# Scaling the sink-attention weights on ScalarE, one tile for all sink columns, and earlier steps from projection to scores

## The chip, the cores and the metric

The kernel runs on one core of a Trainium2 chip. The metric is the device time of one execution in microseconds (us); lower is better. TensorE (PE) does the matmuls and transposes, with its weight loads (PEld) overlapping them; VectorE (DVE), ScalarE (ACT) and GpSimd (POOL) do the rest, and SyncE (SP) issues the weight loads from memory.

## The reference

Two transformer blocks of width 1024 on 256 tokens. The first is an FFN, a mixer of dilated-window and block attention, and an FFN. The second has two layers with modulated norms; the change lies in the mixer of its first layer, sliding-window attention with a sink:

```python
    qkv = h @ w_qkv                       # 16 query heads, 2 key/value heads, 64 wide
    q = partial_rope(rmsnorm_2(q, q_gain), positions)
    k = partial_rope(rmsnorm_2(k, k_gain), positions)
    ...
    s = jnp.where(valid, s, -jnp.inf)
    sink_col = jnp.broadcast_to(sink_logit, s.shape[:-1] + (1,))
    p = jax.nn.softmax(jnp.concatenate([s, sink_col], axis=-1), axis=-1)[..., :-1]
    o = jnp.einsum('bkgqs,bskd->bqkgd', p.astype(vb.dtype), vb)
    ...
    x = x + g1 * (out @ w_o)              # sliding-window layer, then its FFN
```

## The kernel before

Every weight matrix is read once from memory in blocks of sixteen 128x128 tiles (`raw`). ACT rounds a block to a high part (`wh`, line 211, in quarters of 128x512) and DVE subtracts to get the low part (`wl`, line 219). Each product is three matmuls (`mm3`, lines 271 to 273). TensorE's instruction stream is written out by the Python code, and so is every other engine's: a manual schedule, in which each engine runs its list strictly in the order written.

What runs beside the matmuls is a set of coroutines in the list `hooks`. The code that emits matmuls calls `pump()` after every four products (12 matmuls); a pump advances each coroutine by one step and casts at most a quarter or two of a coming weight block. So a step written one pump earlier lands 12 matmuls earlier in TensorE's stream.

The mixer of the sink attention, from 600 us to 679 us, goes so:

- `feat_unit` projects two 128-row column tiles of q, k or v at a time (16 products, four pumps). Five units: (k, q0), (v, q1), (q2, q3), (q4, q5), (q6, q7). Its `evac` calls `shifted`: DVE multiplies by the norm's root (`sh`, line 988), ACT adds the shift (`flat`, line 991), and `operand` follows as a coroutine: TensorE turns the tile (line 1029), ACT squares it (`hsq`, 1046), DVE multiplies by the gain (`ht`, 1047) and reduces (`hss`, 1049), POOL does the rotation and the root (1051 to 1057), TensorE turns it back (1061) and ACT writes `qT` or `kT` (1067, 1065).
- `soft_heads` works on eight pairs of heads, called pair 0 to pair 7 here. `run_heads` starts a pair every second pump when its q tile is ready, and holds at most `most` pairs alive. The steps of a pair: scores on TensorE (line 691, tiles `at`) with mask and row minimum on DVE (`u`, `lo`, line 703); exponentials with row sums on ACT (line 711); reciprocals and scaling by them on DVE (lines 717, 719); the turn of the weights on TensorE (line 726) and copies to `pt` on ACT (line 728); two pumps later the product with the values (line 736), `yh` on ACT (750), then `yl` on DVE (752), and two pumps on the pair is `ready`.
- `out_proj` multiplies by w_o, K tile by K tile: K tile c needs pair c, takes eight products (two pumps), and while pair c is not ready the code only calls `pump()`, with no matmul in between. Here such a pump is called an empty pump.

The PSUM tiles `at` share four banks, which the code hands out as they come free. A tile's first write waits until the readers of the bank's last tile are done. Which tile follows which is in the built program.

A separate coroutine, `two_norms`, takes the roots of two norms, spreads them over the partitions, and after a pause multiplies the residual `xT` by one of them on POOL (line 978), one of eight tiles per pump.

Of the kernel before, what the change touches and what calls it, by code (L numbers as in the profile page):

```python
# [2 lines left out]

# [7 lines left out]
F32 = mybir.dt.float32  # L11
# [7 lines left out]
S = 256  # L19
# [8 lines left out]

SWA_HEADS = 2, 3, (1, 1, 2)
MOBA_HEADS = 6, 2, (1, 1, 1)  # L30
# [127 lines left out]
def hybrid_two_block_kernel(ctx: ExitStack, tc: tile.TileContext, x, w, ada, vecs, rows, pos, consts,  # L158
# [400 lines left out]

    def feat_unit(name, xh, xl, evac, n=S, first=False):  # L560

        wh, wl = W.next(name)
        ps = [mm_ps([128, n]), mm_ps([128, n])]
        order = [(u, kc) for u in range(2) for kc in range(DC)]
        if first:
            order.sort(key=lambda o: o[1])
        for i, (u, kc) in enumerate(order):
            t = u * DC + kc
            mm3(ps[u], wh[:, t], wl[:, t], xh[:, kc, :n], xl[:, kc, :n], kc == 0, kc == DC - 1)
            if i % 4 == 3:  # L570
                pump()
            if i == 11:
                release()
        held.extend((evac, u, ps[u]) for u in range(2))
        if not first:
            release()
# [77 lines left out]
    def soft_heads(pool, n_heads, n_parts, part, y_h, y_l, ready, sink=None, gate=lambda j: True,  # L654
# [6 lines left out]
        cut = 128 + (sink is not None)  # L661
        wide = 384 + 2 * (sink is not None)

        def one(c):
# [15 lines left out]
            for j in js:  # L680
                u[j] = pool.tile([128, n_parts, wide], F32, tag=f"u{n_parts}", bufs=2 * most, name=nm("u"))
                lo[j] = pool.tile([128, 2 * n_parts], F32, tag=f"lo{n_parts}", bufs=2 * most, name=nm("lo"))
                sums[j] = pool.tile([128, 2], F32, tag="sm", bufs=6, name=nm("sm"))
                if sink is not None:
                    nc.vector.tensor_copy(u[j][:, 0, 128:386:257], sink[:, j:j + 1].to_broadcast([128, 2]))
            for g in range(n_parts):
# [22 lines left out]
            for j in js:  # L709
                for tt, sl in ((0, slice(0, cut)), (1, slice(cut, wide))):  # L710
                    nc.scalar.activation(u[j][:, :, sl], u[j][:, :, sl], AF.Exp,
                                         bias=lo[j][:, 2 * g + tt:2 * g + tt + 1],
                                         scale=-1.0, accum_out=sums[j][:, tt:tt + 1])
            yield from pause(gaps[0])
            for j in js:
                rs = pool.tile([128, 2], F32, tag="rs", bufs=6, name=nm("rs"))
                nc.vector.reciprocal(rs, sums[j])
                for tt, sl in ((0, slice(0, 128)), (1, slice(cut, cut + 256))):
                    nc.vector.tensor_scalar(u[j][:, :, sl], u[j][:, :, sl], rs[:, tt:tt + 1], None, op0=ALU.mult)
            yield from pause(gaps[1])  # L720
# [31 lines left out]
            nc.vector.tensor_sub(y_l[:, c], o, y_h[:, c])  # L752
            yield
            yield
# [205 lines left out]
    def two_norms():  # L960
# [14 lines left out]
        fin.spread(r4[:, 0:2], fin.r)  # L975
        yield from pause(14)
        for d in range(DC):
# [4 lines left out]

    def shifted(pool, norm, p, dst, then):

# [9 lines left out]

        hooks.append(rest())

# [16 lines left out]
    with ExitStack() as mix:  # L1013
# [11 lines left out]
        def operand(c, flat):  # L1025
# [21 lines left out]
            nc.vector.tensor_mul(t, p, R[:, at:at + 64].unsqueeze(1).unsqueeze(1).to_broadcast([128, 2, 2, 64]))  # L1047
            yield
            nc.vector.tensor_reduce(ss, sq, axis=mybir.AxisListType.X, op=ALU.add)
# [31 lines left out]
        def keep(two):  # L1081
            def evac(u, p):
                t = mp.tile([128, S], F32, tag="flat", bufs=4, name=nm("flat"))
                shifted(mp, pre, p, t, operand(two[u], t))
            return evac

        for i, two in enumerate(SWA_UNITS):
            feat_unit("wqkv_a_2", xgh, xgl, keep(two), S + 2, first=i == 0)
            if i == 1:
                hooks.append(soft_heads(mp, 16, 1, swa_part, yh, yl, ready, nsink, gate, *SWA_HEADS, lambda: 9 in done))  # L1090
# [177 lines left out]
```

## Time and profile before

| what | value |
|---|---|
| median of three runs | 1189.0 us (1188.76 to 1190.79) |
| the profiled execution: its own time, its span | 1188.8 us, 1187.0 us |
| TensorE busy over the span | 1169.7 us (99%) |
| VectorE, ScalarE, GpSimd busy | 964.4 us, 620.9 us, 129.4 us |
| granted TensorE clock | full speed in all 40 slices |
| from 606.30 to 678.84 us (72.54 us): PE, DVE, ACT, POOL busy | 68.19, 57.91, 51.56, 33.92 us |

The span runs from the first to the last instruction that the profiler saw; about 1.8 us of the execution's time lie outside it. A matmul's record overlaps the next one's, so TensorE counts as busy unless a wait is longer than the overlap. A row by stretch gives the stretch and its length, the busy time of PE, PEld, DVE, ACT and POOL, then the granted clock, the busy share of the DMA engines and GB/s.

### The profile page before, as it was taken

To read this page: it belongs to the slowest core of one execution; us is meant where nothing else is said; L and a number is where in the kernel's file an instruction comes from. 1 tells how busy PE (TensorE), PEld (TensorE's weight loads), DVE (VectorE), ACT (ScalarE), POOL (GpSimd) and SP (SyncE) were. 2 spreads that over 40 slices of the span, in tenths; PEclk is the share of its full clock that TensorE was granted. 3 is DMA by queue.
4 is the path that set the end of the run, shared out by engine and by line. 5 is a ranking of instruction groups with operands and counts; after the bars stand their busy time and mean duration, and the time that the engine had idled before them with its cause. 6 is when DMAs were issued, how large, how long until landed. Compare 5 with 4: busy or idle time off the path is not lost. (4 is left out here: it accounts for less than half of the span.)

```text
span 1187.0 us, 24693 instructions
## 1 busy us (share of the span) xinstructions
PE 1169.7 (99%) x9762; PEld 1132.9 (95%) x9762; DVE 964.4 (81%) x2070; ACT 620.9 (52%) x1324; POOL 129.4 (11%) x166
## 2 busy tenths in 40 slices
PE   8999999999999999999998999999999999999998
PEld 7999999999889999999996899999998889999998
DVE  7989987566567999999878799999968877988752
ACT  5555444455546554554467765444546666545541
POOL 5000001220202200001247010000100002000000
PEclk9999999999999999999999999999999999999999
DMA  8876765535343768876551267767653335755450
GB/s 310 318 276 261 271 241 191 208 126 178 108 142 138 254 253 326 323 277 242 178 185 72 99 252 307 290 264 315 249 191 127 123 131 181 288 218 178 163 203 27
DMA packets 45331, 251.73 MB, mean 212 GB/s; under 512 B 5280, under 2 KB 8096, under 8 KB 21536
## 3 DMA queue, kind: packets, MB, share of 16 engines
q1 hardware_dynamic: 44784, 248.78, 57.2%
q8 instruction: 77, 1.26, 0.4%
q10 hardware_dynamic: 432, 1.38, 0.4%
q14 instruction: 38, 0.31, 0.1%
HBM read 249.09 MB, written 1.05 MB: 211 GB/s over the span
## 5 line engine op out<-in xcount | busy, mean ns | idle before, releaser
L211 ACT CAST wh<-raw 128x512 fp32r<-128x512 f32 (+1 forms) x752 | 420.2, 613 | 265.8 <-issue 138.4
L219 DVE TENSOR_TENSOR wl<-raw,wh 128x512 fp32r<-128x512 f32 x744 | 501.1, 707 | 51.8 <-ACT wh L211 50.5
L271 PE MATMUL mm<-xgh,wh 128*128 128x256 f32 (+1 forms) x1840 | 524.8, 285 | 0.0
L273 PE MATMUL mm<-xgh,wl 128*128 128x256 f32 (+1 forms) x1840 | 519.3, 282 | 0.0
L272 PE MATMUL mm<-xgl,wh 128*128 128x256 f32 (+1 forms) x1840 | 518.0, 282 | 0.0
L271 PEld LDWEIGHTS mm<-xgh,wh 128*128 128x128 f32 x1840 | 347.0, 189 | 7.5 <-issue 7.0
L272 PEld LDWEIGHTS mm<-xgl,wh 128*128 128x128 f32 x1840 | 348.3, 189 | 0.0
L273 PEld LDWEIGHTS mm<-xgh,wl 128*128 128x128 f32 x1840 | 347.1, 189 | 0.2 <-DVE wl L219 0.2
L271 PE MATMUL mm<-ah,wh 128*128 128x256 f32 x704 | 197.1, 280 | 0.0
L272 PE MATMUL mm<-al,wh 128*128 128x256 f32 x704 | 196.7, 279 | 0.0
L273 PE MATMUL mm<-ah,wl 128*128 128x256 f32 x704 | 196.7, 279 | 0.0
L272 PEld LDWEIGHTS mm<-al,wh 128*128 128x128 f32 x704 | 132.2, 188 | 0.0
L271 PEld LDWEIGHTS mm<-ah,wh 128*128 128x128 f32 x704 | 132.0, 188 | 0.1
L273 PEld LDWEIGHTS mm<-ah,wl 128*128 128x128 f32 x704 | 131.9, 187 | 0.0
L340 POOL TENSOR_TENSOR ssq<-ssq,sq 128x256 f32<-128x256 f32 x49 | 41.2, 847 | 688.7 <-ACT sq L335 687.8
L439 DVE SCALAR_TENSOR_TENSOR acc<-ada,cs,acc 128x1024 f32<-128x1024 f32 x84 | 107.5, 1280 | 0.6
L335 ACT ACTIVATE sq<-xT 128x256 f32<-128x256 f32 x49 | 19.7, 412 | 83.3 <-DVE xT L554 74.8
L494 DVE TENSOR_TENSOR tu<-mm,rB 128x256 f32<-128x256 f32 x80 | 33.5, 419 | 23.8 <-PE mm L273 23.7
L507 ACT CAST ah<-a 128x256 fp32r<-128x256 f32 x88 | 35.4, 405 | 20.6 <-DVE a L505 13.5
L500 ACT ACTIVATE sg<-tg,bb 128x256 f32<-128x256 f32 x44 | 22.4, 508 | 32.3 <-DVE bb L498 31.8
L272 PE MATMUL at<-xgl,wh 128*128 128x256 f32 (+1 forms) x128 | 37.2, 291 | 1.6 <-DVE xgl L377 1.4
L509 DVE TENSOR_TENSOR al<-a,ah 128x256 fp32r<-128x256 f32 x88 | 36.5, 419 | 1.9 <-ACT ah L507 1.9
(200 smaller groups left out, 1398.3 us busy)
## 6 DMA issues: line engine op xcount, KB each, us to landing
raw<-in_w SPq DMA_DIRECT2D x185, 1024.0 KB, 5.2
ada<-in_ada SPq DMA_DIRECT2D x96, 512.0 KB, 4.7
raw<-in_w SPq DMA_DIRECT2D x8, 128.0 KB, 4.0
raw<-in_w SPq DMA_DIRECT2D x4, 256.0 KB, 5.2
out<-xT SPq DMA_DIRECT2D x8, 128.0 KB, 2.1
xT<-in_x SPq DMA_DIRECT2D x3, 256.0 KB, 4.3
M<-in_masks ACTq DMA_DIRECT2D x1, 768.0 KB, 4.3
Mstick<-in_masks ACTq DMA_DIRECT2D x1, 386.0 KB, 3.3
```

The costliest lines, as they stand in the source:

```text
L211: nc.scalar.copy(h[:, part], self.raw[i][:, part])
L219: engine.tensor_sub(l[:, part], self.raw[i][:, part], h[:, part])
L271: nc.tensor.matmul(ps, lhsT=lh, rhs=rh, start=start, stop=False)
L272: nc.tensor.matmul(ps, lhsT=lh, rhs=rl, start=False, stop=False)
L273: nc.tensor.matmul(ps, lhsT=ll, rhs=rh, start=False, stop=stop)
L335: nc.scalar.activation(t, src, AF.Square, scale=scale)
L340: nc.gpsimd.tensor_add(self.ssq, self.ssq, t)
L439: nc.vector.scalar_tensor_tensor(self.acc, raw, self.cs[:, kc:kc + 1], self.acc, op0=ALU.mult, op1=ALU.add)
L494: nc.vector.tensor_mul(tu, ps[1][:, :S], norm.r)
L500: nc.scalar.activation(sg, tg, AF.Silu, bias=bb[:, 0:1] if shift else 0.0)
L507: nc.scalar.copy(ah[:, c], a)
L509: nc.vector.tensor_sub(al[:, c], a, ah[:, c])
```

## The change

Six edits, all in or around the sink attention.

1. All sixteen heads get their weights in one tile, `wells`, and both sink columns of all heads are written by one copy before the first pair starts, where before two small copies per pair wrote them.
2. The two reciprocals of a pair come in one pump, and the scaling follows in the next, on ACT (`AF.Copy` with the reciprocal as scale), where before both stood in one pump on DVE. Heads without a sink keep their scaling on DVE, after both reciprocals.
3. The last idle step before `ready` is taken out, for all three users of `soft_heads`.
4. `operand` reduces in the pump in which it squares; ACT's `flat` is issued as soon as `sh` is (the turn still comes two pumps on); the first unit's tiles are released one pump sooner (`free=7`).
5. `SWA_HEADS` lets four pairs live at once (before, three).
6. `two_norms` pauses 20 pumps (before, 14) ahead of the eight products on POOL.

```diff
-SWA_HEADS = 2, 3, (1, 1, 2)
+SWA_HEADS = 2, 4, (1, 1, 2)
...
-    def feat_unit(name, xh, xl, evac, n=S, first=False):
+    def feat_unit(name, xh, xl, evac, n=S, first=False, free=11):
...
-            if i == 11:
+            if i == free:
                 release()
...
+        if sink is not None:
+            wells = pool.tile([128, n_heads, wide], F32, name="wells")
+            nc.vector.tensor_copy(wells[:, :, 128:386:257], sink.unsqueeze(2).to_broadcast([128, n_heads, 2]))
...
-                u[j] = pool.tile([128, n_parts, wide], F32, tag=f"u{n_parts}", bufs=2 * most, name=nm("u"))
+                if sink is None:
+                    u[j] = pool.tile([128, n_parts, wide], F32, tag=f"u{n_parts}", bufs=2 * most, name=nm("u"))
+                else:
+                    u[j] = wells[:, j:j + 1]
...
-                if sink is not None:
-                    nc.vector.tensor_copy(u[j][:, 0, 128:386:257], sink[:, j:j + 1].to_broadcast([128, 2]))
...
+            rs = {j: pool.tile([128, 2], F32, tag="rs", bufs=6, name=nm("rs")) for j in js}
             for j in js:
-                rs = pool.tile([128, 2], F32, tag="rs", bufs=6, name=nm("rs"))
-                nc.vector.reciprocal(rs, sums[j])
+                nc.vector.reciprocal(rs[j], sums[j])
+            if sink is not None:
+                yield
+            for j in js:
                 for tt, sl in ((0, slice(0, 128)), (1, slice(cut, cut + 256))):
-                    nc.vector.tensor_scalar(u[j][:, :, sl], u[j][:, :, sl], rs[:, tt:tt + 1], None, op0=ALU.mult)
+                    if sink is None:
+                        nc.vector.tensor_scalar(u[j][:, :, sl], u[j][:, :, sl], rs[j][:, tt:tt + 1], None, op0=ALU.mult)
+                    else:
+                        nc.scalar.activation(u[j][:, :, sl], u[j][:, :, sl], AF.Copy, scale=rs[j][:, tt:tt + 1])
...
             nc.vector.tensor_sub(y_l[:, c], o, y_h[:, c])
             yield
-            yield
             ready.add(c)
...
-        yield from pause(14)
+        yield from pause(20)
...
-    def shifted(pool, norm, p, dst, then):
+    def shifted(pool, norm, p, dst, then, at_once=False):
...
-        hooks.append(rest())
+        g = rest()
+        if at_once:
+            next(g)
+            g = chain(pause(1), g)
+        hooks.append(g)
...
             nc.vector.tensor_mul(t, p, R[:, at:at + 64].unsqueeze(1).unsqueeze(1).to_broadcast([128, 2, 2, 64]))
-            yield
             nc.vector.tensor_reduce(ss, sq, axis=mybir.AxisListType.X, op=ALU.add)
...
-                shifted(mp, pre, p, t, operand(two[u], t))
+                shifted(mp, pre, p, t, operand(two[u], t), True)
...
-            feat_unit("wqkv_a_2", xgh, xgl, keep(two), S + 2, first=i == 0)
+            feat_unit("wqkv_a_2", xgh, xgl, keep(two), S + 2, first=i == 0, free=7)
```

What this does to the order shows in three places. In the rows, the line numbers of the changed kernel are larger by 5 to 14, and the number behind a name tells one buffer from another.

**TensorE where the projections end and the output projection begins.** In the kernel before, the last turn of the projections' K loop is followed by three empty pumps; these are the second and third of them (values of pair 1, the turns of q6 and q7, scores of pair 3, the turns back of q4 and q5), and then w_o's first product:

```order
L736 MATMUL at_8365<-pt_8316,vt_7689 64x128
L1029 MATMUL at_8375<-C,flat_8320 128x128 x2
L1029 MATMUL at_8386<-C,flat_8325 128x128 x2
L691 MATMUL at_8415<-kT_7687,qT_7688 128x128
L691 MATMUL at_8416<-kT_7687,qT_7688 128x128
L691 MATMUL at_8415<-kT_7687,qT_7688 128x256
L691 MATMUL at_8416<-kT_7687,qT_7688 128x256
L1061 MATMUL at_8425<-C,ht_8223 128x128 x2
L1061 MATMUL at_8429<-C,ht_8234 128x128 x2
L271 MATMUL mm_8338<-yh_7690,wh_7992 128x256
L272 MATMUL mm_8338<-yl_7691,wh_7992 128x256
L273 MATMUL mm_8338<-yh_7690,wl_7993 128x256
```

In the changed kernel, scores of pair 2 and values of pair 1 are all that stands between the last projection product and w_o's first:

```order
L274 MATMUL mm_8174<-xgh,wl_7898 128x258
L696 MATMUL at_8318<-kT_7687,qT_7688 128x128
L696 MATMUL at_8319<-kT_7687,qT_7688 128x128
L696 MATMUL at_8318<-kT_7687,qT_7688 128x256
L696 MATMUL at_8319<-kT_7687,qT_7688 128x256
L747 MATMUL at_8352<-pt_8289,vt_7689 64x256
L747 MATMUL at_8352<-pt_8295,vt_7689 64x256
L747 MATMUL at_8352<-pt_8289,vt_7689 64x128
L747 MATMUL at_8352<-pt_8295,vt_7689 64x128
L272 MATMUL mm_8348<-yh_7690,wh_8007 128x256
L273 MATMUL mm_8348<-yl_7691,wh_8007 128x256
```

Scores of pair 3 and the four turns have moved behind w_o's first products: there is one empty pump where there were three.

**ScalarE around the third K tile of w_o.** Before, ACT goes from yh of pair 2 over the copies of pair 3, the exponentials of pair 4, a weight cast and the last two q tiles to yh of pair 3 and the copies of pair 4 (the first of them is the last row):

```order
L750 CAST yh_7690<-at_8540 128x256
L728 COPY pt_8550<-at_8546 128x384
L728 COPY pt_8556<-at_8552 128x384
L711 ACTIVATE u_8507,sm_8509<-u_8507,lo_8508 128x129
L711 ACTIVATE u_8507,sm_8509<-u_8507,lo_8508 128x257
L711 ACTIVATE u_8511,sm_8513<-u_8511,lo_8512 128x129
L711 ACTIVATE u_8511,sm_8513<-u_8511,lo_8512 128x257
L211 CAST wh_8447<-raw_7996 128x512
L1067 ACTIVATE qT_7688<-at_8586 128x256
L1067 ACTIVATE qT_7688<-at_8590 128x256
L750 CAST yh_7690<-at_8594 128x256
L728 COPY pt_8604<-at_8600 128x384
```

In the changed kernel, the scaling of pair 3 and the exponentials of pair 4 come first, then yh of pair 2 and the copies of pair 3:

```order
L730 ACTIVATE wells<-wells,rs_8493 128x128
L730 ACTIVATE wells<-wells,rs_8493 128x256
L730 ACTIVATE wells<-wells,rs_8494 128x128
L730 ACTIVATE wells<-wells,rs_8494 128x256
L716 ACTIVATE wells,sm_8498<-wells,lo_8497 128x129
L716 ACTIVATE wells,sm_8498<-wells,lo_8497 128x257
L716 ACTIVATE wells,sm_8500<-wells,lo_8499 128x129
L716 ACTIVATE wells,sm_8500<-wells,lo_8499 128x257
L761 CAST yh_7690<-at_8534 128x256
L739 COPY pt_8544<-at_8540 128x384
L739 COPY pt_8550<-at_8546 128x384
```

Behind these rows follow the last two q tiles, the scaling of pair 4, the exponentials of pair 5, yh of pair 3 and the copies of pair 4, with no weight cast among them. Four scaling instructions a pair have come into ACT's list, and the exponentials of a pair now stand ahead of the copies of the pair before it, where they stood behind them.

**TensorE in the same stretch of the changed kernel.** Three empty pumps stand together here, ahead of the third K tile; the first brings values of pair 2, the turn of pair 3, and scores of pair 5 and the turns back of q6 and q7 (the first six rows); the third brings values of pair 3, the turn of pair 4 and scores of pair 6:

```order
L696 MATMUL at_8560<-kT_7687,qT_7688 128x128
L696 MATMUL at_8561<-kT_7687,qT_7688 128x128
L696 MATMUL at_8560<-kT_7687,qT_7688 128x256
L696 MATMUL at_8561<-kT_7687,qT_7688 128x256
L1074 MATMUL at_8570<-C,ht_8411 128x128 x2
L1074 MATMUL at_8574<-C,ht_8429 128x128 x2
L747 MATMUL at_8589<-pt_8544,vt_7689 64x256
L747 MATMUL at_8589<-pt_8550,vt_7689 64x256
L747 MATMUL at_8589<-pt_8544,vt_7689 64x128
L747 MATMUL at_8589<-pt_8550,vt_7689 64x128
L737 MATMUL at_8595<-C,wells 128x128 x3
L737 MATMUL at_8601<-C,wells 128x128 x3
```

Scores of pair 6 and then w_o's third K tile follow. In the built program, the second score tile of pair 5 (at_8561) lies in the bank of the first turned tile of pair 3, and that of pair 6 in the bank of the first turned tile of pair 4, so each waits for a copy to `pt` on ACT. Before, this place had two empty pumps, and scores of pair 5 behind the turn of pair 4.

## Rows read from the trace of the kernel before

**Rows 1.** The page's first part: busy us, share, instructions.

```profile
PE 1169.7 (99%) x9762; PEld 1132.9 (95%) x9762; DVE 964.4 (81%) x2070; ACT 620.9 (52%) x1324; POOL 129.4 (11%) x166
```

**Rows 2.** Stretches to last projection product, w_o, third K tile, FFN: busy us (instructions).

```profile
606.30:631.30 25.00, 23.73 (x194) 21.93 (x192) 19.93 (x69) 18.88 (x53) 17.14 (x34) 1.00 0.36 128
631.30:639.57 8.27, 6.21 (x47) 4.04 (x47) 6.89 (x31) 5.04 (x17) 7.10 (x14) 1.00 0.00 1
639.57:653.10 13.53, 12.71 (x106) 10.16 (x104) 12.48 (x49) 10.32 (x33) 9.69 (x17) 1.00 0.22 79
653.10:678.84 25.74, 25.54 (x213) 22.35 (x211) 18.62 (x65) 17.32 (x50) 0.00 (x0) 1.00 0.23 83
```

**Rows 3.** Timeline of TensorE: start, us, instruction, idle time before it and its releaser.

```profile
618.89 0.44 PE L1061 MATMUL at<-C,ht 128*128 128x128 f32 x2 [0.45 <-POOL ht L1057]
...
627.42 0.63 PE L1029 MATMUL at<-C,flat 128*128 128x128 f32 x4 [0.82 <-DVE lo L703]
...
638.31 0.92 PE L691 MATMUL at<-kT,qT 64*128 64x128 f32 x6 [1.15 <-DVE ht L1047]
...
651.03 0.41 PE L726 MATMUL at<-C,u 128*128 128x128 f32 x2 [0.43 <-ACT yh L750]
...
667.15 0.87 PE L736 MATMUL at<-pt,vt 128*64 128x256 f32 x8
667.98 0.68 PE L726 MATMUL at<-C,u 128*128 128x128 f32 x3
668.85 0.67 PE L726 MATMUL at<-C,u 128*128 128x128 f32 x3 [0.20 <-DVE u L719]
```

**Rows 4.** Groups of ScalarE, 606.3 to 678.84: busy us, mean ns, idle before.

```profile
L211 ACT CAST wh<-raw 128x512 fp32r<-128x512 f32 x28 | 16.5, 616 | 2.3 <-PE mm L272 2.3
L711 ACT ACTIVATE u<-u,lo 128x257 f32<-128x257 f32 x16 | 8.0, 502 | 0.0
...
L711 ACT ACTIVATE u<-u,lo 128x129 f32<-128x129 f32 x16 | 6.4, 402 | 0.6 <-DVE lo L703 0.6
...
L750 ACT CAST yh<-at 128x256 fp32r<-128x256 f32 x8 | 3.0, 372 | 7.2 <-PE at L736 7.2
...
L1003 ACT ACTIVATE xgh<-xT,G 128x256 fp32r<-128x256 f32 x2 | 0.9, 506 | 1.3 <-DVE xT L1001 1.3
```

**Rows 5.** Timeline of ScalarE: one pair's exponentials, then casts, q tiles and copies.

```profile
641.97 0.49 ACT L728 COPY pt<-at 128x384 f32<-128x384 f32 x1
642.34 0.42 ACT L711 ACTIVATE u<-u,lo 128x129 f32<-128x129 f32 x1
...
644.12 1.13 ACT L211 CAST wh<-raw 128x512 fp32r<-128x512 f32 x2
...
649.63 0.61 ACT L211 CAST wh<-raw 128x512 fp32r<-128x512 f32 x1
650.14 0.64 ACT L1067 ACTIVATE qT<-at 128x256 f32<-128x256 f32 x2
650.67 0.37 ACT L750 CAST yh<-at 128x256 fp32r<-128x256 f32 x1
```

**Rows 6.** Groups of VectorE instructions by form, the same stretch.

```profile
L703 DVE CUSTOM_DVE_ANT_0 u<-at,Mswa,nsink 128x256 f32<-128x256 f32 x16 | 7.7, 481 | 0.0
L719 DVE TENSOR_SCALAR u<-u,rs 128x256 f32<-128x256 f32 x16 | 6.1, 383 | 0.0
...
L719 DVE TENSOR_SCALAR u<-u,rs 128x128 f32<-128x128 f32 x16 | 5.3, 334 | 0.6
```

**Rows 7.** Timeline of POOL and VectorE: roots' products, xT's products, a scaling.

```profile
614.32 1.75 POOL L1057 TENSOR_TENSOR ht<-ht,hrr 128x256 f32<-128x256 f32 x2
...
648.84 2.63 POOL L978 TENSOR_TENSOR xT<-xT,rB 128x256 f32<-128x256 f32 x3
...
649.87 1.02 DVE L719 TENSOR_SCALAR u<-u,rs 128x128 f32<-128x128 f32 x2
```

More of the change, by code (lines that the diff above doesn't have):

```diff
@@ L2 @@
 from contextlib import ExitStack
+from itertools import chain
 import numpy as np
```

## The prediction

> **What bounds the kernel now.** I read the page's busy times first: TensorE is busy for 99% of the span [rows 1], so a gain can only be time in which TensorE waits, and a loss only a new wait. Of the 17 us that it idles, the busy time by stretch puts 4.35 us into the sink mixer, 606.3 to 678.84 us [rows 2]: 1.3 while the projections run, 2.1 in the three empty pumps before w_o, 0.8 until w_o's third K tile, 0.2 after. The rest of the program keeps its instructions, but for the attentions of the first block, below. So the most that the change can save is near 4.4 us, and a little more for waits that hide under overlapping matmul records: of the two wait rows at 651.03 and 668.85, the idle shown is 0.43 and 0.20, while from the turn at 667.98 to the latter it is 0.87 us for three transposes.
>
> TensorE's timeline then tells what it waits for: the roots from POOL (618.89), a PSUM bank held by DVE (627.42), DVE behind ACT (638.31), ACT and DVE at 651.03, DVE's scaling at 668.85 [rows 3]. No single engine is to blame: in the 72.54 us DVE is busy for 57.9 and ACT for 51.6 [sums of rows 2], and each stands idle waiting for TensorE (ACT 7.2 us ahead of `yh` alone [rows 4]). The question is what ACT's 21 us of slack become when the scaling moves there.
>
> **What a scaling costs.** Before, a pair costs DVE two 128-wide and two 256-wide multiplications, 2 x (0.334 + 0.383) = 1.43 us, 11.4 us for eight pairs [rows 6]. On ACT no row shows a 128- or 256-wide Copy with a pointer scale from SBUF to SBUF in f32. The nearest is L1003, 256 wide with a pointer scale, 0.506 us; the exponentials, 257 and 129 wide, take 0.502 and 0.402 [rows 4]. But instructions overlap: a pair's four exponentials with their four sum reads run from 642.34 to 644.12, 1.78 us, and the four sum reads take a good 0.09 each of it [rows 5], so 0.40 and 0.30 from start to start. A pair's scaling is then 2 x 0.70 = 1.40 us. Bounds: with no overlap 2 x (0.50 + 0.40) = 1.80; at the pace of q tiles read from PSUM, 0.53 us for two of 256 columns [rows 5], less 0.10 for the narrower ones, 2 x (0.27 + 0.17) = 0.88. I take 1.40, since width and operands match there. Eight pairs add 11.2 us, so ACT rises from 51.6 to 62.8 of some 72 us.
>
> The Trainium skill ("ScalarE: Activation LUTs", "Rules for kernel authors") speaks against this edit: multiplications belong on VectorE, ScalarE being for transcendentals. The rows agree as to a single instruction, 0.383 against some 0.50 us. By that page's price ("What ACT_TABLE_LOAD costs": 0.186 us, 0.093 for a pointer, 0.833 ns a column, 0.093 overlapped) a pair would be an estimated 1.38 us; the sum would stay as it is.
>
> **Up to the last projection product.** The turns of k and q0 come a pump sooner, and scores of pair 0 two pumps sooner. A pump with 12 matmuls takes 1.5 us: the last stretch's 25.74 us less its wait (0.7), four value products at 0.83 (667.15 to 667.98), two scores at 0.92 and three turns at 0.7, over twelve pumps [rows 2, 3]. The engines behind don't quite keep up: (a) POOL's products with the roots of k and q0 ended at 616.07 [rows 7]; with the first turn one pump sooner they end near 614.6, while TensorE is there two pumps sooner, at 612.9, and waits about 0.95 us, as the first of the two is there sooner. (b) pair 0's turn waits 0.45 us for the scaling: DVE's reciprocal stands behind two `hss` that wait for ACT's squares, which stand behind the exponentials. (c) the turns of q4 and q5 need the bank of pair 0's turned tile; its copy stands on ACT behind pair 1's exponentials (1.78), two `flat` (0.8) and a cast (0.5), which costs 1.45 us. (d) values of pair 0 wait 0.6 us for the bank of q2, whose copy stands behind pair 1's scaling. Together 3.45 us, against before's two waits (1.27 us idle [rows 3], some 1.7 from start to start). The turn of pair 1 (0.7) and values of pair 0 (0.8) now stand ahead of the last projection product too. It ends at 631.3 + 1.75 + 1.5 = 634.5 us.
>
> **From there to w_o's third K tile.** Two empty pumps fewer: w_o begins sooner than at 639.57. But ACT first waits for DVE: q6 and q7 are read from PSUM behind yl of pair 0 and four masked minima (two at 0.48 [rows 6], two narrower), about 0.4 until TensorE's first scores are there, 1.4 for the minima and 0.5 for yl and `sh`: 2.3 us in all. From 636.8 on ACT has work without a break, in this order (start to start, from [rows 5]): two `flat` 0.80, shift cast 0.10, yh 0.30, exponentials 1.78, cast 0.51, two q tiles 0.53, squares 0.54 after a wait of 0.4 for TensorE, cast 0.51 (5.5 so far); scaling 1.40, exponentials 1.78, cast 0.51, two copies 0.74, cast 0.51 (10.4); scaling 1.40, exponentials 1.78, yh 0.30, two copies 0.74 (14.6); a wait of 1.05, since scores of pair 5 need the bank of pair 3's first turned tile and the last q tiles are turned behind those scores, q tiles 0.53, scaling 1.40, exponentials 1.78, yh 0.30, one copy 0.48 (20.2). Then 0.75 us for the rest of pair 6's scores, which wait for that bank. The third K tile starts at 636.8 + 20.2 + 0.75 = 657.8 us, where it started at 653.10 [rows 2]. TensorE's own work in between is only some 16.5 us (four pumps 6.0, five scores 4.6, three value products 2.5, three turns 2.1, turning q4 to q7 1.3); the other 6.8 are new waits, in the three empty pumps above all. Scores of pair 6 (0.92 [rows 3]) are then done, which before came later, so the loss is 3.8 us.
>
> **The tail.** Before, 25.74 us from there to the FFN's first product. Off go pair 6's scores 0.92, the wait near 668 (0.7 from start to start) and some 0.5 for four switches between kinds of matmul; on comes 0.5 for pair 7's scores, which again wait for a copy behind exponentials. 24.1 us, so the mixer ends at 681.9, 3.1 us late.
>
> **The rest costs nothing.** The one sink copy replaces sixteen on DVE, which has slack now. The eight products on POOL now follow the last root in one row, 0.88 us each by three of before [rows 7], 7 us; they end some 20 us before w_o's first tile is added to xT. The freed step before `ready` lets the second dilated pair start a pump sooner, where TensorE has matmuls at every pump; in the block attention it drops an empty pump at the end, whose waits are for the scaling. If that cover is wrong, a few tenths either way.
>
> Sum: the profiled execution's own 1188.8 + 3.1 = 1191.9; its time lies 0.2 under the median, so 1192.1, rounded to 1192.0 us.
>
> **Rivals.** (1) ACT's lag doesn't reach TensorE, because most copies come early enough: then the stretch costs TensorE's own 16.5 us, the tail 23.6, and the end is 674.6, 4.2 us sooner: 1184.6 us. For it: ACT waits 7.2 us for TensorE before `yh` now [rows 4]. Against: its chain would have to shrink from 21.0 to 14.2 us, more than all three scalings in it; it breaks even with before at 3.1 us less. (2) No change, 1189.4 us: scaling at 0.88 a pair takes 1.6 us from the chain, and waits (a) to (d) as before take 1.7. (3) What is freed on DVE counts most. Beside POOL's products DVE's two multiplications at 649.87 take 1.02 us [rows 7], against 0.72 by the mean [rows 6]. Ending these collisions would remove the wait at 651.03, 1.3 us from start to start: 1187.5 us, inside no change. The Trainium skill ("SBUF — State Buffer", "Who interferes with whom") says that such a DVE instruction and a GpSimd one block each other fully; the rows fit that, but TensorE then waits for ACT there. (4) ACT's casts come so late that w_o or the FFN waits for weights too: 1195 us; it decides if ACT is still behind at pair 7, when its exponentials end and it has 1.8 us a pair to spare.
>
> **How the numbers follow.** About 0.2%, 2.4 us, can be told from no change here: faster is below 1186.6, slower above 1191.4. My forecast gets 0.49, (4) 0.08, (2) 0.22, (3) 0.08, (1) 0.13. The forecast's own range is 1190.0 to 1194.0: 0.88 or 1.80 us a pair (-1.9, +1.4), waits ahead of w_o by half a us. The whole range, 1187.4 to 1195.0, takes in (2) to (4) up to their times and leaves out (1) and the far side of (4).
>
> **What would show it.** Right: ACT busy near 63 us in the stretch, without its waits before `yh`; TensorE idle for several us before w_o's third K tile, released by ACT's copies and scaling; the scaling at 0.4 and 0.5 us; no wait near 668. Wrong: TensorE idle under 4 us in the mixer, or waits that end on DVE or POOL.

## The result and the profile after

The changed kernel takes 1196.67 us (median of six, 1194.03 to 1197.2), the kernel before 1188.88 us in the same comparison: ratio 1.0058, 95% interval 1.0047 to 1.0068. It is slower by 7.8 us, where 3.1 were forecast, and lies 1.7 us above the whole range (1187.4 to 1195.0).

The page's first part of the changed kernel, beside [rows 1]:

```profile
PE 1174.4 (98%) x9762; PEld 1136.0 (95%) x9762; DVE 953.7 (80%) x2023; ACT 630.7 (53%) x1356; POOL 127.3 (11%) x166
```

VectorE has lost 10.7 us and ScalarE gained 9.8. TensorE runs the same 9762 matmuls, but is busy 4.7 us longer: matmuls themselves took longer somewhere. The stretches of [rows 2] after the change, busy us and instructions of PE, PEld, DVE, ACT and POOL, then granted clock, DMA share and GB/s:

```profile
606.30:635.03 28.73, 26.45 (x210) 23.40 (x208) 20.25 (x65) 22.33 (x64) 17.20 (x35) 1.00 0.32 111
635.03:636.77 1.74, 1.74 (x19) 1.01 (x17) 1.74 (x8) 0.00 (x0) 1.66 (x6) 1.00 0.00 0
636.77:660.15 23.38, 18.00 (x129) 13.04 (x127) 13.12 (x60) 20.50 (x70) 13.61 (x23) 0.96 0.13 46
660.15:686.58 26.43, 26.43 (x204) 24.12 (x203) 13.54 (x40) 18.80 (x51) 0.00 (x0) 0.90 0.22 81
```

The FFN starts at 686.58 us, where it started at 678.84: 7.7 us late, the whole loss. The third stretch shows ScalarE busy for 20.5 of 23.4 us and TensorE idle for 5.4. The last two show something that no row of before has: a granted clock below 1.00 (0.96 and 0.90). TensorE's timeline says where the waits are, beside [rows 3]:

```profile
614.76 0.44 PE L1074 MATMUL at<-C,ht 128*128 128x128 f32 x2 [0.50 <-POOL ht L1070]
...
629.50 0.81 PE L1043 MATMUL at<-C,flat 128*128 128x128 f32 x4 [1.11 <-ACT pt L739]
...
632.06 0.87 PE L747 MATMUL at<-pt,vt 128*64 128x256 f32 x8 [0.28 <-ACT qT L1080]
...
641.82 0.66 PE L1043 MATMUL at<-C,flat 128*128 128x128 f32 x4 [1.18 <-ACT qT L1080]
...
652.28 0.92 PE L696 MATMUL at<-kT,qT 64*128 64x128 f32 x6 [1.53 <-ACT pt L739]
...
658.58 1.64 PE L696 MATMUL at<-kT,qT 64*128 64x128 f32 x6 [1.53 <-ACT pt L739]
660.15 0.58 PE L272 MATMUL mm<-yh,wh 128*128 128x256 f32 x1
...
665.46 0.87 PE L747 MATMUL at<-pt,vt 128*64 128x256 f32 x8
...
668.23 0.38 PE L272 MATMUL mm<-yh,wh 128*128 128x256 f32 x1
...
671.15 0.87 PE L747 MATMUL at<-pt,vt 128*64 128x256 f32 x8
```

The long waits end on ScalarE's copies and q tiles, the last two in the three empty pumps, at the scores of pairs 5 and 6. And the third K tile's 24 matmuls take from 660.15 to 665.46, 5.31 us, where the fourth's take 2.92 (668.23 to 671.15). By stretch of 3 us (TensorE's busy time is the first number behind the length, the granted clock the third from the end):

```profile
652.00:655.00 3.00, 2.36 (x18) 1.40 (x18) 1.78 (x9) 1.61 (x6) 3.00 (x5) 1.00 0.00 0
655.00:658.00 3.00, 1.90 (x12) 0.97 (x8) 0.24 (x2) 3.00 (x13) 0.00 (x1) 1.00 0.00 0
658.00:661.00 3.00, 2.42 (x10) 1.78 (x11) 1.25 (x8) 3.00 (x9) 0.00 (x0) 0.58 0.01 3
661.00:664.00 3.00, 3.00 (x16) 3.00 (x16) 1.96 (x7) 2.07 (x9) 0.00 (x0) 0.50 0.24 68
664.00:667.00 3.00, 3.00 (x22) 2.46 (x21) 0.00 (x0) 0.52 (x2) 0.00 (x0) 0.79 0.69 289
```

In the 6 us before it falls, TensorE was busy for 4.26; then the clock goes from its upper level (2.4 GHz) to the lower (1.2 GHz) for some 7 us. The Trainium skill ("TensorE: Matmul & The Clock Gate", Part 1) says that this clock is set by how busy the array has lately been. The fall behind the waits fits that. It does not come each time: in the kernel before, TensorE was busy for 3.94 of the 6 us from 632.5 on, and the clock of that execution stayed up:

```profile
632.50:638.50 6.00, 3.94 (x29) 2.42 (x29) 4.72 (x23) 4.76 (x17) 5.86 (x11) 1.00 0.01 1
```

The other executions of the changed kernel have no trace, but their times fit a fall that is worth some 3 us: the one with a mean granted clock of 0.999 took 1194.03 us, the five at 0.996 or 0.997 took 1195.77 to 1197.2.

ScalarE's timeline and its groups, beside [rows 4, 5]:

```profile
637.94 0.91 ACT L1001 ACTIVATE flat<-sh,shb 128x256 f32<-128x256 f32 x2 [3.07 <-DVE sh L998]
...
648.34 1.50 ACT L730 ACTIVATE wells<-wells,rs 128x128 f32<-128x128 f32 x4
649.73 0.41 ACT L716 ACTIVATE wells<-wells,lo 128x129 f32<-128x129 f32 x1
...
657.80 0.35 ACT L761 CAST yh<-at 128x256 fp32r<-128x256 f32 x1
658.05 0.84 ACT L739 COPY pt<-at 128x384 f32<-128x384 f32 x2
```

```profile
L730 ACT ACTIVATE wells<-wells,rs 128x256 f32<-128x256 f32 x16 | 8.0, 501 | 0.0
...
L730 ACT ACTIVATE wells<-wells,rs 128x128 f32<-128x128 f32 x16 | 6.4, 401 | 1.4 <-DVE rs L722 1.4
```

A pair's scaling runs from 648.34 to 649.73, 1.39 us: the price taken (1.40). ScalarE's chain begins at 637.94, after an idle 3.07 us, because VectorE had weights and minima of pair 2 ahead of `sh` (VectorE's timeline):

```profile
634.47 1.29 DVE L220 TENSOR_TENSOR wl<-raw,wh 128x512 fp32r<-128x512 f32 x2
635.67 0.42 DVE L763 TENSOR_TENSOR yl<-at,yh 128x256 fp32r<-128x256 f32 x1
636.07 0.35 DVE L708 CUSTOM_DVE_ANT_0 wells<-at,Mswa,nsink 128x128 f32<-128x128 f32 x1
...
637.50 0.41 DVE L998 TENSOR_TENSOR sh<-mm,rB 128x256 f32<-128x256 f32 x1
```

### The profile page after: what moved, and what is told of

The parts are those of the page before. It is cut to its first block, busy times and chain, and to the rows that moved or that the text cites. A ratio compares the mean times of both kernels' runs of the same rounds, so it can differ in the third digit from the quotient of the medians.

```text
span 1194.7 us, 24646 instructions
## 1 busy us (share of the span) xinstructions
PE 1174.4 (98%) x9762; PEld 1136.0 (95%) x9762; DVE 953.7 (80%) x2023; ACT 630.7 (53%) x1356; POOL 127.3 (11%) x166
## 5 line engine op out<-in xcount | busy, mean ns | idle before, releaser
L508 ACT CAST ah<-a 128x256 fp32r<-128x256 f32 x88 | 35.4, 405 | 20.6 <-DVE a L506 13.5
L272 PE MATMUL mm<-yh,wh 128*128 128x256 f32 x128 | 38.3, 300 | 0.0
```

What stands on the lines that cost most here:

```text
L272: nc.tensor.matmul(ps, lhsT=lh, rhs=rh, start=start, stop=False)
L508: nc.scalar.copy(ah[:, c], a)
```

## The experiments

Theory 1, from the prediction: ScalarE's queue, longer by the scaling, makes TensorE wait. Theory 2, formed after the first four runs: the earlier steps of the fourth edit cost as much by themselves. Theory 3: the extra pump of the second edit puts exponentials ahead of copies, and that order is what costs. All runs, in the order in which they were made:

| kernel | us, median (range) | ratio to before (95%) |
|---|---|---|
| scale_dve | 1195.95 (1194.53 to 1196.14) | 1.0052 (1.0038 to 1.0065) |
| no_yield | 1193.6 (1193.35 to 1195.08) | 1.0037 (1.0024 to 1.0049) |
| act_alone | 1193.88 (1191.52 to 1194.61) | 1.0033 (1.0021 to 1.0044) |
| fill | 1194.56 (1193.46 to 1196.07) | 1.0045 (1.0032 to 1.0057) |
| early_alone | 1192.69 (1191.18 to 1193.37) | 1.0023 (1.0014 to 1.0033) |
| late_steps | 1193.33 (1192.7 to 1194.3) | 1.0028 (1.0017 to 1.0039) |
| most3 | 1193.13 (1192.28 to 1195.02) | 1.0031 (1.002 to 1.0042) |
| sinks_ready | 1188.13 (1187.58 to 1188.64) | 0.9986 (0.9978 to 0.9995) |
| act_same | 1196.21 (1194.55 to 1196.68) | 1.0051 (1.0039 to 1.0064) |
| dve_extra | 1189.22 (1188.13 to 1189.58) | 0.9995 (0.9986 to 1.0004) |
| sinks_ready_20 | 1189.39 (1187.65 to 1191.96) | 0.9997 (0.9989 to 1.0006) |
| sinks_ready_red | 1190.93 (1189.49 to 1192.8) | 1.0013 (1.0004 to 1.0021) |
| dve_14 | 1196.81 (1196.3 to 1197.36) | 1.0069 (1.0056 to 1.0082) |
| dve_most3 | 1195.18 (1194.09 to 1195.98) | 1.0054 (1.0041 to 1.0066) |
| dve_late | 1190.26 (1189.29 to 1190.69) | 1.0009 (1.0 to 1.0018) |
| ready_alone | 1188.38 (1187.78 to 1190.11) | 0.9997 (0.9988 to 1.0006) |

The kernel before had medians of 1188.93 to 1189.42 us beside these. What a kernel costs is given below as its distance to the kernel before of the same comparison, and two kernels are compared by these distances (the changed kernel's is 7.8 us).

**scale_dve.** The changed kernel, scaling on VectorE:

```diff
-                        nc.scalar.activation(u[j][:, :, sl], u[j][:, :, sl], AF.Copy, scale=rs[j][:, tt:tt + 1])
+                        nc.vector.tensor_scalar(u[j][:, :, sl], u[j][:, :, sl], rs[j][:, tt:tt + 1], None, op0=ALU.mult)
```

> The changed kernel with the scaling back on VectorE, everything else as changed (the extra pump between reciprocals and scaling too). Theory 1, ScalarE's queue: four pairs' scalings of 1.40 us (5.6 us) leave ScalarE's chain ahead of w_o's third K tile, so the two waits of 1.8 us there shrink to under half a us each, the clock stays at full speed and the time falls by 5 to 9 us, to 1188 to 1192 us. Rival, the order: the early steps and the fourth pair put the empty pumps into one place, whatever engine scales; then the time stays over 1194 us.

It took 1195.95 us, 6.5 over the kernel before: theory 1 as the one cause falls, and the 1.3 us between it and the changed kernel can't be told from nothing (their intervals overlap). The copies' waits are gone and others have come, as TensorE's and VectorE's timelines of this kernel show:

```profile
626.74 1.13 PE L734 MATMUL at<-C,wells 128*128 128x128 f32 x4 [1.54 <-ACT wells L716]
...
652.85 0.44 PE L734 MATMUL at<-C,wells 128*128 128x128 f32 x2 [0.36 <-DVE wells L727]
...
654.26 0.44 PE L734 MATMUL at<-C,wells 128*128 128x128 f32 x2 [0.42 <-DVE wells L727]
```

```profile
626.31 1.73 DVE L727 TENSOR_SCALAR wells<-wells,rs 128x128 f32<-128x128 f32 x4
...
646.79 1.11 DVE L727 TENSOR_SCALAR wells<-wells,rs 128x128 f32<-128x128 f32 x4
...
651.29 2.91 DVE L727 TENSOR_SCALAR wells<-wells,rs 128x128 f32<-128x128 f32 x4
```

The first turn now waits 1.54 us for its weights, whose scaling VectorE only begins at 626.31, and at 651.29 us four multiplications take 2.91 us instead of 1.11, while POOL is busy with xT. Behind both places the clock falls, as stretches of this kernel show:

```profile
628.00:629.00 1.00, 0.81 (x4) 0.84 (x5) 1.00 (x6) 0.53 (x2) 0.00 (x0) 0.50 0.00 0
...
655.00:660.00 5.00, 4.68 (x25) 2.62 (x22) 3.02 (x15) 3.00 (x13) 1.84 (x3) 0.50 0.00 0
```

By stretches of half a us it is low for some 10.2 us in all. At the rate of the K tiles above (2.4 of 5.31 us lost) that is an estimated 4.6 us at most, the larger part of what this kernel loses.

**no_yield.** The changed kernel without the extra pump:

```diff
-            if sink is not None:
-                yield
```

> The changed kernel with reciprocals and scaling in one pump, still on ScalarE, so that the copies of a pair stand ahead of the next pair's exponentials and a pair is ready one pump sooner. Theory 1 (the amount of work on ScalarE decides): the chain keeps its 4.9 us a pair and the time stays within 3 us of the changed kernel's, 1194 to 1198 us. Rival (the order on ScalarE decides, copies behind exponentials): the waits for copies before w_o's third K tile go, the clock stays up, 1190 us or less.

1193.6 us, between the two: 3.6 us come back and 4.2 stay. Its profile has no fall of the clock in the mixer, so the 4.2 are lost without one; how much of the 3.6 is the order and how much the clock isn't told apart.

**act_alone.** The kernel before, with the second edit alone:

```diff
+            if sink is not None:
+                yield
...
-                    nc.vector.tensor_scalar(u[j][:, :, sl], u[j][:, :, sl], rs[:, tt:tt + 1], None, op0=ALU.mult)
+                        nc.scalar.activation(u[j][:, :, sl], u[j][:, :, sl], AF.Copy, scale=rs[j][:, tt:tt + 1])
```

> The kernel before with the second edit alone: reciprocals in one pump, scaling in the next, on ScalarE. Theory 1: ScalarE gets the same 11.2 us without the earlier steps and is late by as much, 1192 to 1197 us. Rival, the order of the earlier steps and the fourth pair is at fault: within 1.5 us of the kernel before, 1187.5 to 1190.5 us.

1193.88 us, as theory 1 has it. TensorE's and ScalarE's timelines show why:

```profile
650.86 1.25 PE L742 MATMUL at<-pt,vt 128*64 128x256 f32 x8 [2.37 <-ACT pt L734]
...
671.35 1.27 PE L742 MATMUL at<-pt,vt 128*64 128x256 f32 x8 [2.20 <-ACT pt L734]
```

```profile
646.14 1.50 ACT L725 ACTIVATE u<-u,rs 128x128 f32<-128x128 f32 x4
647.53 0.39 ACT L711 ACTIVATE u<-u,lo 128x129 f32<-128x129 f32 x1
...
650.33 0.85 ACT L734 COPY pt<-at 128x384 f32<-128x384 f32 x2
```

The copies stand behind a scaling and four exponentials. Right behind each of these two waits the clock falls (stretches of 5 us, granted clock 0.70 and 0.74):

```profile
650.00:655.00 5.00, 4.14 (x22) 2.79 (x22) 0.00 (x0) 4.30 (x11) 0.00 (x0) 0.70 0.00 0
...
670.00:675.00 5.00, 3.65 (x19) 2.75 (x20) 1.98 (x4) 5.00 (x14) 0.00 (x0) 0.74 0.20 84
```

**fill.** The changed kernel with matmuls that add zeros where TensorE waits:

```diff
                     for j in js:
+                        if sink is not None and c in (5, 6) and t == 0 and j == js[1]:
+                            for _ in range(12):
+                                nc.tensor.matmul(accs[0][:, 0], lhsT=accs[4], rhs=y_h[:, 0], start=False, stop=False)
```

> The changed kernel with twelve matmuls by a zero tile, added onto one of the open sums of w_o, between the two score tiles of pair 5 and of pair 6, where TensorE waits 1.8 us each for a copy on ScalarE. Twelve take 1.4 us, inside the wait. If the fall of the granted clock to half speed from 658 to 665 us comes of these waits and costs 3 us, the clock stays at full speed and the time is 1193.2 to 1194.2 us. Rival, the fall has another cause, or the waits before 650 us: the clock falls as before and the time is 1196 to 1197.5 us.

1194.56 us, between both expectations; of five executions the two with a mean granted clock of 1.000 took 1193.46 and 1194.03, as expected for a clock that stays up, the other three 1194.56 to 1196.07. The profiled one (1196.07) is of the latter (by stretch):

```profile
643.00:647.00 4.00, 4.00 (x22) 4.00 (x23) 3.60 (x13) 3.68 (x13) 2.52 (x6) 0.57 0.50 209
647.00:655.00 8.00, 8.00 (x67) 6.63 (x66) 3.13 (x14) 6.75 (x23) 7.92 (x14) 1.00 0.00 0
655.00:662.00 7.00, 6.50 (x45) 4.22 (x42) 2.46 (x14) 5.70 (x20) 1.12 (x2) 1.00 0.01 4
662.00:667.00 5.00, 5.00 (x43) 4.37 (x44) 2.87 (x12) 4.60 (x17) 0.00 (x0) 1.00 0.45 151
```

Where the waits are filled, 647 to 667 us, the clock stays up; it falls now at 643, behind a wait for a q tile that is left (1.17 us before 642.88). In this execution it also falls at the program's start, from 8 to 16 us, so the mean clock doesn't speak of the mixer alone. That the fall comes of the waits fits, and its price too, but it isn't settled by one profile.

All 18 profiles together say more. In eleven the clock falls in the mixer, each time behind waits of TensorE, and these kernels lose 1.7 to 7.9 us. Of the seven without, six lie within 1.3 us of the kernel before, and no_yield loses 4.2. What decides whether a wait brings a fall stays open: no_yield and the kernel before have waits over 1 us without one.

**early_alone, late_steps.** The fourth edit alone on the kernel before, and the changed kernel without it:

```diff
-            yield
             nc.vector.tensor_reduce(ss, sq, axis=mybir.AxisListType.X, op=ALU.add)
...
+                shifted(mp, pre, p, t, operand(two[u], t), True)
...
+            feat_unit("wqkv_a_2", xgh, xgl, keep(two), S + 2, first=i == 0, free=7)
```

> The kernel before with the fourth edit alone (earlier steps from projection to scores), scaling on VectorE as before. With the scaling back on VectorE the changed kernel still took 1196 us, so ScalarE's load alone isn't the cause. New theory 2: the earlier steps bring pair 0 and 1 ahead of what VectorE and ScalarE have done, and the last projection product ends 3.5 us later though only 1.5 us of work was brought ahead of it: 1190.5 to 1193 us. Rival, theory 1 as amended: the earlier steps are harmless while the scaling keeps its one pump, 1187.5 to 1189.5 us.

> The changed kernel without the fourth edit. Theory 2 (early steps cost some 2 us and the clock's fall comes with them): 1189 to 1192 us, no better than the second edit alone, which took 1191.5 to 1194.6. Rival (ScalarE's queue alone): 1194 us or more.

1192.69 us: theory 2 holds, the earlier steps cost 3.4 us with the scaling where it was. They cost as much where the clock stays up: the three executions with a mean clock of 1.000 took 1191.18 to 1191.99 us, the six such of the kernel before beside them 1187.08 to 1188.83. late_steps took 1193.33 us: 3.8 come back, but 4.0 stay, between both expectations; so there are two causes. In early_alone's timeline of TensorE:

```profile
624.89 1.41 PE L727 MATMUL at<-C,u 128*128 128x128 f32 x6 [1.23 <-DVE u L720]
...
641.60 0.41 PE L1065 MATMUL at<-C,ht 128*128 128x128 f32 x2 [1.84 <-DVE yl L753]
```

Both end on VectorE: pair 0's turn on its scaling, and the turn back of a q tile on a bank that `yl` reads.

**most3.** The changed kernel with three pairs alive, and **dve_most3**, **dve_14**, the same and a pause of 14 on top of scale_dve:

```diff
-SWA_HEADS = 2, 4, (1, 1, 2)
+SWA_HEADS = 2, 3, (1, 1, 2)
```

```diff
-        yield from pause(20)
+        yield from pause(14)
```

> The changed kernel with three pairs alive at most, as before. If the fourth pair is what puts exponentials ahead of the copies that TensorE waits for, the waits at pair 5 and 6 go and the time is 1191 us or less. If the scaling's extra pump and the early steps decide, a pair that must wait for a place only moves the empty pumps: within 1.5 us of the changed kernel, 1195 to 1198 us.

> The changed kernel with the scaling back on VectorE and three pairs alive. With the scaling on ScalarE the third pair's limit gave 3.5 us back. If the fourth pair costs by stacking exponentials on ScalarE ahead of copies, whoever scales: 1191.5 to 1193.5 us, the cost of the early steps alone. Rival, it costs through the clock or POOL: 1194.5 us or more.

> The changed kernel with the scaling back on VectorE, which took 1195.95 us, and the pause before the products on POOL back at 14 pumps. In that run four multiplications of a scaling took 2.91 us at 651.29 us beside these products, where 1.1 us is their usual time, and TensorE waited for them four times. If POOL's products are what spoils the scaling on VectorE, 1194 us or less; rival, the early steps and the fourth pair are enough: 1195 to 1197 us.

most3 took 1193.13 us, halfway: the fourth pair costs 4.0 us beside the other edits. On top of scale_dve it is 0.3, inside the spread. dve_14 took 1196.81 us, as its rival had it, but doesn't settle whether POOL's products keep scale_dve slow. The pause of 14 did not take them away from the scaling, as the timelines of VectorE and POOL in dve_14 show:

```profile
651.97 2.80 DVE L727 TENSOR_SCALAR wells<-wells,rs 128x128 f32<-128x128 f32 x4
```

```profile
652.48 2.87 POOL L985 TENSOR_TENSOR xT<-xT,rB 128x256 f32<-128x256 f32 x4
```

The four multiplications take 2.80 us there, and TensorE waits for them four times as in scale_dve. A run in which the two don't meet is missing.

**act_same, dve_extra.** The second edit taken apart on the kernel before: scaling on ScalarE without the extra pump, and the extra pump with scaling on VectorE:

```diff
+            if sink is not None:
+                yield
             for j in js:
                 for tt, sl in ((0, slice(0, 128)), (1, slice(cut, cut + 256))):
```

> The kernel before with the scaling on ScalarE, in the same pump as the reciprocals: the second edit without its extra pump. In the run with the second edit alone, TensorE waited twice for 2.4 and 2.2 us for copies to pt that stood on ScalarE behind the next pair's exponentials, which the extra pump had put ahead of them. Theory 3 (the extra pump's order is the cause): both waits go, 1188.5 to 1190.5 us. Rival, theory 1 (the load on ScalarE): the same 11.2 us on ScalarE cost as much as there, 1192.5 to 1195 us.

> The kernel before with an extra pump between the reciprocals and the scaling, which stays on VectorE: the second edit without its move to ScalarE. Theory 3 (order): the copies stand behind the next pair's exponentials here too, 1191.5 to 1194.5 us. Rival, theory 1 (load): no more than a pump's delay hidden by empty pumps, within 1 us of the kernel before, 1188.3 to 1190.3 us.

1196.21 and 1189.22 us: theory 3 falls, theory 1 holds for the second edit. The pump alone costs nothing, the engine alone 6.9 us, and with the pump 4.5. The 6.9 lie 1.2 us above theory 1's range; in the profile of act_same the clock is low for some 10 us from 637 on, so the clock has a part in them too.

**dve_late.** scale_dve without the fourth edit.

> The changed kernel with the scaling back on VectorE and without the early steps (so with one sink copy, the extra pump, no idle pump before ready, four pairs, the pause of 20). If the early steps are the second cause beside the scaling on ScalarE, what is left is free, 1188 to 1190 us. Rival, the fourth pair or POOL's products cost by themselves: 1191 us or more.

1190.26 us, 0.3 above the range for "free". With the earlier steps the same kernel takes 1195.95 (scale_dve), so they are what keeps it slow. All edits but the second's engine and the fourth cost 1.3 us together, which is at the edge of what can be told from nothing (interval from 1.0000).

**sinks_ready, ready_alone, sinks_ready_20, sinks_ready_red.** The kernel before with the first and third edits; with the third alone; and both with the sixth, or with the part of the fourth that takes the `yield` before the reduction out:

```diff
             nc.vector.tensor_sub(y_l[:, c], o, y_h[:, c])
             yield
-            yield
             ready.add(c)
```

> The kernel before with the first and third edits alone: one copy for all sink columns, and the idle pump before a pair is ready taken out. Both theories: no engine gets more to do, and a pair is ready one pump sooner, so that an empty pump or two go ahead of w_o; 1187 to 1189.5 us. Rival: w_o's first K tiles only meet the same waits (pair after pair is limited by its own chain), no change within 0.7 us, or the empty pumps were needed and it is slower.

> The kernel before with the third edit alone (no idle pump before ready). With the sink copy it took 1188.13 us. If the gain is the pump: 1187.5 to 1188.6 us. If the gain is the sixteen small copies off VectorE: within 0.5 us of the kernel before.

> The kernel before with the first, third and sixth edits (one sink copy, no idle pump before ready, the products of xT six pumps later). The first and third took 1188.13 us. If the products on POOL slow VectorE's scaling where TensorE waits for it, six pumps later moves them beside other work: POOL is then free at 648 us but busy ahead of 660 us. Expected within 0.7 us of 1188.1; a rival, that they now fall on the empty pumps ahead of w_o's third K tile, 1189 us or more.

> The kernel before with the first and third edits and the part of the fourth that reduces in the pump in which it squares (the turn back and the scores come a pump sooner, while ScalarE's shift and the release of the first unit stay). If all of the fourth edit's cost of 3.4 us is in pairs that start before VectorE and ScalarE are done, half of the step costs about half: 1189 to 1190.5 us. Rival, a pump of slack is there: 1186.5 to 1188 us.

sinks_ready took 1188.13 us, 0.9986 (0.9978 to 0.9995) of before, a gain of 0.6 to 2.6 us by the interval. Among the executions with a mean clock of 1.000 the medians are 1187.95 and 1188.28, so a good part of the gain lies in how seldom its clock fell. Its stretches to the last projection product, w_o, its third K tile and the FFN:

```profile
606.30:630.85 24.55, 23.84 (x196) 22.14 (x194) 18.82 (x64) 18.73 (x54) 16.56 (x32) 1.00 0.37 130
630.85:636.32 5.47, 4.30 (x36) 2.79 (x35) 5.30 (x26) 3.52 (x11) 4.22 (x10) 1.00 0.00 1
636.32:653.14 16.82, 15.05 (x117) 11.40 (x116) 13.15 (x48) 12.14 (x41) 13.25 (x22) 1.00 0.20 64
653.14:678.64 25.50, 25.30 (x213) 22.20 (x211) 18.58 (x62) 17.35 (x50) 0.00 (x0) 1.00 0.23 84
```

w_o starts 3.2 us sooner than in [rows 2], and the third K tile at the same time: the third edit moves the empty pumps, and little more. ready_alone's time (1188.38) was as expected, but its ratio can't be told from no change. With the sixth edit the time is 1189.39, as the rival had it, and the gain is gone; among the executions with a mean clock of 1.000 the two kernels take the same (1187.65 to 1188.52 and 1187.58 to 1188.36). Half a step of the fourth (sinks_ready_red) took 1190.93 us, 0.4 above its range, and costs 2.8: most of what the whole edit costs, not half.

## Why the prediction was wrong

The direction and the mechanism ahead of w_o's third K tile were right; the size was not, and one cause was put too low.

- **A scaling at 1.40 us a pair, and ScalarE busy for 62.8 us.** Right: 1.39, and 61.6 us in the stretches above.
- **Up to the last projection product, 634.5 us.** Near: 635.03, with the roots' spread 0.23 us later from the start on (601.72 against 601.49). Waits (a), (c) and (d) stand in the timeline with the releasers named (POOL's `ht`, the copy to `pt`, the q tile), each shorter than forecast (0.50, 1.11 and 0.28 us idle); (b) is nearly nothing. That the end came out is in part luck: TensorE's idle time there grew by 1.0 us and its busy time by 2.7, where 1.75 and 1.5 were forecast.
- **ScalarE first waits 2.3 us, then has work from 636.8 on.** Mis-sized: it waited 3.07 us and began at 637.94, 1.1 us late; 0.8 of it is the longer wait. Left out were 1.29 us of weights on VectorE ahead of `yl` and the minima.
- **The chain of 20.2 us.** Right: from 637.94 to the end of the first copy at about 658.5, 20.6 us.
- **The third K tile at 657.8 us.** It began at 660.15: 1.1 from the start, 0.4 from the chain and the release, and the rest of pair 6's scores took 1.57 (658.58 to 660.15) instead of 0.75, at the lower clock.
- **"24.1 us" for the tail.** This is the step that failed. It was taken from rows at full clock, and took 26.43. The third K tile at the lower clock costs 5.31 - 2.92 = 2.4 us. With 0.8 for the scores the clock takes 3.2 us, and 3.1 + 1.1 + 0.4 + 3.2 = 7.8, the loss of 7.7 us to rounding. The forecast asked what each new wait costs, and not what happens to the clock behind them; no rival had it, so the range ended too soon. That the waits brought the fall is argued from the profiles, not shown by a run that changes nothing else.
- **ScalarE's chain as the main cause.** Half right. On the kernel before, the engine alone costs 6.9 us and with its pump 4.5. But the earlier steps cost 3.4 alone, and what each costs depends on the other: with late steps the engine costs 2.7 us (dve_late to late_steps), with early steps 1.3 (scale_dve to the changed kernel), and the early steps cost 5.2 us without the engine's move and 3.8 with it. The forecast gave the waits ahead of w_o, most of them from the early steps, 1.75 us. Why scaling on VectorE meets waits as long as on ScalarE once the steps are early is shown only in part: pair 0's turn waits for VectorE, and pairs reach VectorE's queue behind the minima and reductions of the q tiles. In scale_dve the clock adds an estimated 4.6 us at most, and the meeting with POOL's products has a part that no run took out.
- **"The rest costs nothing."** Right for the first and third edits (a gain of about a us, in part the clock's); for the sixth no cost of its own can be told. The fourth pair, for which the sum had no term of its own, costs some 4.0 us beside the other edits.

Rival (1), the lag hidden, rival (2), no change, and rival (3), collisions freed, found nothing in the changed kernel's time; rival (2)'s own terms (1.6 us off the chain, waits of 1.7 instead of 3.45) give some 1188.8 us and not 1189.4. Rival (4)'s time was near the truth for another reason.

## What to carry to other kernels

A forecast that adds waits to TensorE must ask next whether its clock stays up behind them: here some 4 us of new waits were followed by a fall that cost 3 more. Moving work to the engine with the most slack is judged by that engine's queue at the one place where TensorE waits, not by its sum over the stretch: ScalarE had 21 us of slack and still became the bound. And edits that each shift a schedule need testing both alone and taken out of the whole: the second edit and the early steps cost 4.5 and 3.4 us alone, which happens to add up to the whole loss, but taking the engine's move or the early steps out gives back 1.3 and 3.8.

## What the runs showed of the hardware

- The granted clock falls in some executions of one kernel and not in others. The kernel before, profiled at 1.000, had executions between 0.996 and 1.000 in the comparison with early_alone (1187.08 to 1192.36 us; those at 1.000 took 1187.08 to 1188.83, those at 0.996 1190.64 to 1192.36). Where in the program it fell in those isn't known. The profiles show two places: the mixer, in eleven of 18, and the program's start at 8 to 16 us, in five (fill, early_alone, sinks_ready, sinks_ready_20, dve_late). A comparison of kernels that differ by a us or two has to look at both.
- Scaling by a pointer on ScalarE costs the same as an exponential of that width: 0.401 and 0.501 us beside 0.395 and 0.500 for one column more.
- Four multiplications on VectorE took 2.91 us beside POOL's products (2.80 in dve_14) and 1.11 without. The Trainium skill ("SBUF — State Buffer", "Who interferes with whom") says that such a multiplication and a GpSimd instruction can block each other for a whole instruction; the rows agree. TensorE waited for these four, 1.5 us in four pieces in scale_dve; what it would gain if they didn't meet was not run.
